# One offset for all blocks of a run, a fourth product in two halves, and other room for a tile's gate weights in a hybrid decoder layer

## The chip, the cores and the metric

The kernel runs on one core of a Trainium2 chip. What counts is the device time of one execution in microseconds (us). The engines that matter are TensorE (PE, with its weight loads as PEld), VectorE (DVE), ScalarE (ACT), GpSimd (POOL) and SyncE (SP), whose queue issues most DMAs.

## The reference

One decoder layer on x of 512 tokens by 1024 channels, in float32: a SwiGLU feed-forward half, a mixer (dilated attention beside a state-space model), and a second SwiGLU half, each between two RMS norms.

```python
h = rms_norm(x, ffn1_pre_g)
x = x + 0.5 * rms_norm(swiglu(h, ffn1_w_in, ffn1_w_out), ffn1_post_g)
h = rms_norm(x, mix_pre_g)
q, k, v, u = split(h @ w_mix_in)
mixed = concat([dilated_attention(q, k, v), s5_mixer(u, ...)]) @ w_mix_out
x = x + rms_norm(mixed, mix_post_g)
h = rms_norm(x, ffn2_pre_g)
x = x + 0.5 * rms_norm(swiglu(h, ffn2_w_in, ffn2_w_out), ffn2_post_g)

def swiglu(x, w_in, w_out):
    gate, up = split(x @ w_in)          # 1024 -> 2 x 2816
    return (silu(gate) * up) @ w_out    # 2816 -> 1024
```

## The kernel before

**Numbers in two parts.** A float32 matrix product is made as three TensorE products: every operand is cut into a high half (a cast to fp32r) and a low half (the rest), and hi·hi, hi·lo and lo·hi are added in one PSUM bank. For weights `wsplit` does it: ScalarE casts `wraw` to `whi` (L117), then DVE or POOL (`pool=True`) subtracts and writes `wlo` (L119). `mm` (L144) issues every product, so nearly all of TensorE's rows have that line, and tiles tell them apart. `mm3` issues the three products.

**Rooms and offsets.** `halves` (L99) gives the next `whi` and `wlo` tiles, out of four rooms each, 1088 elements wide. Of these 1024 are used, from element 0, or from element 16 (`APART`) with `apart=True`. `wraw` has three rooms. A room is free again when the last product that reads it is done. `pad` (L107) takes bytes in a pool so that the tiles behind it lie at other addresses.

**Feed-forward halves.** The 22 tiles of 128 hidden channels are made in two ways. The first 8 (6 in the second half) go one by one, as a gate and an up product with 512 moving columns (`gu`, function `products`). The others go two at a time in `pair` (L598), by a scheme with seven block products in place of eight: `times` (L584) issues one block, 24 products of 128x128 weights with 256 moving columns, into the banks `wx`, `wy` or `wq`. The moving operands are tiles `bh`/`bl` and `tq`, made ahead by `sums`. Between stretches of pairs stand the output products (`yo`, 512 columns); a stretch of pairs between two of them is called a run here. There are five runs, of 3, 4, 3, 3 and 2 pairs; `lead` is true in the first pair of each. In this pair the first block's weights (`a11`) are cut with `apart=not lead`, at element 0; all other blocks at element 16.

**Boundaries.** `boundary` (L273) joins two parts of the layer: it makes the last four k-tiles of the output product (`yt`, 256 columns, the "tail", two halves of the tokens), the norms, the residual, and the first products of the next part (`first`, 256 columns). Between them stand `st` (sums for a norm, 2 columns) and `rp` (spreading the norm's factor, 128 columns). The tail's first products, into the two banks `b2`, are issued by the loop at L330 to L334: k-tiles 0 to 2 for both banks, then k-tile 3. The four chunks of weights for `first` take all four rooms of `whi` and `wlo`.

**Second half.** In `swiglu_half` (L643) tiles 0 and 1 come from the boundary; tile 2 is the third, whose gate weights are loaded by `products(2)`. Pool `fin` holds `gp`, `wx`, `wsum`, `wa` and the `tq` tiles `tq00` to `tq21` of `sums`. The `hooks` put small work between products: `xt` transposes, `st` and `rp` of the boundary's last norm.

**Order.** Instructions wrapped in `fix` keep the order in which they are written; the framework's scheduler orders the others on each engine by its own estimates, and gives each tile its place and its waits.

Of the kernel before, what the change touches and what calls it, by code (L numbers as in the profile page):

```python
# [9 lines left out]
F32R = mybir.dt.float32r  # L10
# [7 lines left out]
P = 128  # L18
S = 512
D = 1024  # L20
KD = D // P
# [11 lines left out]
HT = S // 2  # L33
# [11 lines left out]
class Layer:  # L45
# [227 lines left out]
    def boundary(self, y, tail, ipost, half, inext, chunks):  # L273
# [3 lines left out]
        w = [self.load(c, (KD, P), pool=i % 2 == 1, apart=True) for i, c in enumerate(chunks)]  # L277
        tw = lambda i, m, k: self.tw[m // 2][i].rearrange("p (m k j) -> p m k j", k=NT, j=P)[:, m % 2, k]
        hs = [slice(0, HT), slice(HT, S)]
# [5 lines left out]
        bank, acc = [None], [self.acct(), self.acct()]  # L285
# [43 lines left out]
        b2 = [self.bank("yt")[:, :HT] for _ in range(2)]  # L329
        for ks in (range(NT - 1), (NT - 1,)):  # L330
            for m in range(2):
                for k in ks:
                    th, tl = tail(k)
                    self.mm3(b2[m], tw(0, m, k), tw(1, m, k), th[:, hs[0]], tl[:, hs[0]], k == 0, k == NT - 1)  # L334
        for m in range(2):
            gather(0, m, 1, b2[m].unsqueeze(1))
        squares(0, 0, 2, V)
        for m in range(2, KD):
            b = product(0, m)
            if m % 2 or m > 5:  # L340
                m, n = (m - 1, 2) if m < 6 else (m, 1)
# [3 lines left out]
        for m in range(KD):  # L345
            b = product(1, m)
# [157 lines left out]
    def seven(self, fin, w_in, ig, r, ah, al):  # L504

        nc, V = self.nc, self.nc.vector
        more = [fin]  # L510
        wsum = lambda: more[0].tile([P, 1024], F32, name="wsum", tag="wsum", bufs=3)
        wx = lambda: fin.tile([P, 1024], F32, name="wx", tag="wx", bufs=2)
        gp = lambda: fin.tile([P, 1024], F32, name="gp", tag="gp", bufs=2)
        tq = []
        v4 = lambda t: t.rearrange("p (k c) -> p k c", c=HT)
        blocks = []

        def sums(early=False):

            q = [[gp(), gp()], [wx(), wx()]]  # L520

            def scaled(i):
                for j in range(2):
                    c = slice(j * HT, (j + 1) * HT)
                    for k in range(4):
                        V.scalar_tensor_tensor(out=v4(q[i][j])[:, k], in0=self.x(4 * i + k)[:, c],
                                               scalar=self.g(ig, 4 * i + k), in1=r[:, c], op0=ALU.mult, op1=ALU.mult)
                return q[i]

            b11, b12 = scaled(0)  # L530
            b21, b22 = scaled(1)
            more[0] = (yield) or fin
            self.pad(more[0], 192)
            tq.extend([more[0].tile([P, 1024], F32R, name="tq", tag=f"tq{i}{j}") for j in range(2)] for i in range(3))
            n1, n2, t4 = wsum(), wsum(), wsum()
            V.tensor_tensor(out=n1, in0=b11, in1=b12, op=ALU.subtract)
            yield
            bh, bl = [self.b16(n, F32R) for n in ("bh", "bl")] if early else (None, None)
            v = lambda t, i: t.rearrange("p (q k) c -> p q (k c)", q=4)[:, i]

            def plain(*ts):
                for t in ts:
                    i = len(blocks)
                    blocks.append((v(bh, i), v(bl, i)))
                    self.split(*blocks[i], t)

            if early:
                plain(b11)
            V.scalar_tensor_tensor(out=n2, in0=n1, scalar=-1.0, in1=b22, op0=ALU.mult, op1=ALU.subtract)
            if early:  # L550
                plain(b21)
            yield
            V.scalar_tensor_tensor(out=t4, in0=n2, scalar=-1.0, in1=b21, op0=ALU.mult, op1=ALU.subtract)
            self.split(*tq[0], n2)
            t3 = wsum()
            V.tensor_tensor(out=t3, in0=b22, in1=b12, op=ALU.subtract)
            yield
            if early:
                plain(b22, n1)
            yield  # L560
            self.split(*tq[1], t3)
            yield
            self.split(*tq[2], t4)
            if not early:
                yield
                bh, bl = [self.b16(n, F32R) for n in ("bh", "bl")]
                plain(b11, b21, b22, n1)
            yield

        def block(f, up, kh):  # L570
            if up:
                t = wx() if kh else more[0].tile([P, 1024], F32, name="wa", tag="wa")
            else:
                t = self.wp.tile([P, 1024], F32, name="wraw", tag="wraw", bufs=3)
            src = w_in[f + NF * up:f + NF * up + 2, :, kh * S:(kh + 1) * S].rearrange("f p c -> p f c")
            nc.sync.dma_start(out=t.rearrange("p (f c) -> p f c", f=2), in_=src)
            return t

        def cut(t, pool=False, apart=True):
            hi, lo = self.halves(apart)  # L580
            self.wsplit(t, hi, lo, pool)
            return hi, lo

        def times(bank, w, xb, first):  # L584
            for g in range(2):
                for k in range(4):
                    c, m = slice(k * HT, (k + 1) * HT), slice((4 * g + k) * P, (4 * g + k + 1) * P)
                    st = first and g == 0 and k == 0
                    for i, (wi, xi) in enumerate(((0, 0), (0, 1), (1, 0))):
                        self.mm(bank[:, g * HT:(g + 1) * HT], lhsT=w[wi][:, m], rhs=xb[xi][:, c],  # L590
                                start=st and i == 0, stop=g == 1 and k == 3 and i == 2, skip_group_check=True)

        def keep(bank):
            t = self.tmp("kp")
            nc.scalar.copy(out=t, in_=bank)
            return t

        def pair(f, lead=False, late=False):  # L598
            (b11, b21, b22, n1), (n2, t3, t4) = blocks, tq
            add = lambda x, z, t: V.tensor_tensor(out=t, in0=x, in1=z, op=ALU.add)  # L600
            p2 = lambda t: t.rearrange("p (f c) -> p f c", f=2)
            half = lambda t, h: t[:, :, h * HT:(h + 1) * HT]
            gt = p2(gp())
            X = self.bank("wx")
            a11 = block(f, 0, 0)
            times(X, cut(a11, apart=not lead), b11, True)
            s1 = keep(X)
            a12 = block(f, 0, 1)
            h12 = cut(a12, True)
            Y = self.bank("wy")  # L610
            times(Y, h12, b21, True)
            V.tensor_tensor(out=half(gt, 0), in0=p2(Y), in1=p2(s1), op=ALU.add)
            a21, a22 = block(f, 1, 0), block(f, 1, 1)
            c3 = wsum()
            add(a11, a21, c3)
            c2 = wsum()
            add(c3, a22, c2)
            times(X, cut(c2), n2, False)
            s2 = keep(X)
            c1 = wsum()  # L620
            add(a21, a22, c1)
            Q = self.bank("wq")
            times(Q, cut(c1), n1, True)
            q = keep(Q)
            times(X, cut(c3), t3, False)
            V.tensor_tensor(out=q, in0=X, in1=q, op=ALU.add)
            add(c2, a12, c2)
            times(Q, cut(c2), b22, False)
            V.tensor_tensor(out=half(gt, 1), in0=p2(Q), in1=p2(s2), op=ALU.add)
            nc.scalar.activation(out=gt, in_=gt, func=AF.Silu)  # L630
            times(X, cut(a22, True), t4, False)
            s = f % RING
            dst = lambda t, h: half(t.pair(slice(s, s + 2)), h)
            for h, u in ((1, q), (0, X)):
                V.scalar_tensor_tensor(out=half(gt, h), in0=p2(u), scalar=-1.0, in1=half(gt, h), op0=ALU.mult, op1=ALU.mult)
                if late:
                    self.split(dst(ah, h), dst(al, h), half(gt, h))
            if not late:
                self.split(ah.pair(slice(s, s + 2)), al.pair(slice(s, s + 2)), gt)

        return sums, pair

    def swiglu_half(self, first, scope):  # L643
# [3 lines left out]
        w_in, w_out, w_tail = (self.a["w2" + t] for t in "iot")  # L647
        fin = scope.enter_context(self.tc.tile_pool(name="fin", bufs=1))
        hook = self.tokens_first(fin)
        o0, _, r, late = first  # L650
        ah, al = self.ktiles("ah", F32R), self.ktiles("al", F32R)
        o = {f: o0[2 * f:2 * f + 2] for f in range(len(o0) // 2)}
# [4 lines left out]
        def products(f):  # L657
            o[f] = []
            for i, c in enumerate((f, NF + f)):
                w = self.load(w_in[c], (KD, P), pool=i == 1)  # L660
                b = self.bank("gu")
                self.mmk(b, w, self.xh, self.xl, hooks=hooks.get((f, i), {}))
                o[f].append(b)
# [833 lines left out]
```

## Time and profile before

| | |
|---|---|
| time, median of 3 runs | 931.43 us (930.51 to 931.89) |
| the profiled execution's own time | 930.17 us |
| its span, first to last instruction | 928.3 us |
| PE busy | 912.5 us (98%), 6162 products |
| DVE, ACT, POOL busy | 650.9, 442.4, 214.1 us |
| mean granted TensorE clock | 0.997 |
| HBM read, written | 96.13 MB, 9.70 MB |

Times in the profile are microseconds from the span's start. The page groups instructions by line, engine and tiles. The chain that ended last is followed back from the last instruction, at each step to what released it; in order of time, each piece has a start, a length, and the number of instructions merged in it. In a timeline a row has start, length (several instructions of one kind are merged, with their count), engine, line, operation, `out<-in` tiles and shapes; the idle time before it and what ended it stand in brackets. In the table of windows the columns are the stretch, its length, the busy time of PE, PEld, DVE, ACT and POOL with the number of instructions, the granted clock, the DMA engines' busy share, and GB/s. A TensorE row's length is longer than the gap to the next start, since products are pipelined: the pace is read from starts, or from a chain piece's length over its count.

### The profile page before, as it was taken

To read this page: it belongs to the slowest core of one execution; us is meant where nothing else is said; L and a number is where in the kernel's file an instruction comes from. 1 tells how busy PE (TensorE), PEld (TensorE's weight loads), DVE (VectorE), ACT (ScalarE), POOL (GpSimd) and SP (SyncE) were. 2 spreads that over 40 slices of the span, in tenths; PEclk is the share of its full clock that TensorE was granted. 3 is DMA by queue.
4 is the path that set the end of the run, shared out by engine and by line. 5 is a ranking of instruction groups with operands and counts; after the bars stand their busy time and mean duration, and the time that the engine had idled before them with its cause. 6 is when DMAs were issued, how large, how long until landed. Compare 5 with 4: busy or idle time off the path is not lost.

```text
span 928.3 us, 15349 instructions
## 1 busy us (share of the span) xinstructions
PE 912.5 (98%) x6162; PEld 815.1 (88%) x6162; DVE 650.9 (70%) x1071; ACT 442.4 (48%) x685; POOL 214.1 (23%) x127
## 2 busy tenths in 40 slices
PE   9999999999999999999999999899999999999997
PEld 7887789998999989978777899788899989998995
DVE  6999685755577666758898568698357457745856
ACT  6263764552355543525746554473255414541542
POOL 0423202222222134500000025422222212221321
PEclk9999999999999999999999999999999999999999
DMA  8223662324231252292322441245223322332222
GB/s 271 94 69 114 204 239 88 108 90 133 83 120 41 68 195 80 91 232 94 114 69 73 158 134 47 80 148 181 91 92 115 114 91 91 114 114 91 92 91 90
DMA packets 47734, 106.81 MB, mean 115 GB/s; under 512 B 7824, under 2 KB 11152, under 8 KB 47120
## 3 DMA queue, kind: packets, MB, share of 16 engines
q1 hardware_dynamic: 46080, 102.21, 34.1%
q10 hardware_dynamic: 1584, 3.63, 1.1%
q8 instruction: 48, 0.79, 0.3%
q14 instruction: 22, 0.18, 0.1%
HBM read 96.13 MB, written 9.70 MB: 114 GB/s over the span
## 4 chain that ended last, share of the span: by engine, by line
PE 82%; DVE 4%; DMA 1%; issue 1%; ACT 1%; POOLq 0%; POOL 0%; DVEq 0%; SPq 0%; ACTq 0%
PE yo L144 21%; PE wx L144 18%; PE wq L144 9%; PE yt L144 6%; PE gu L144 5%; PE wy L144 5%; PE first L144 5%; PE prj L144 4%; PE prv L144 2%; PE mo L144 2%; PE st L144 1%; PE ys L144 1%; DMA w1d<-w1s 1%; PE pt L1087 1%; DVE wlo L119 1%
## 5 line engine op out<-in xcount | busy, mean ns | idle before, releaser
L117 ACT CAST whi<-wraw 128x1024 fp32r<-128x1024 f32 (+5 forms) x129 | 125.0, 976 | 167.3 <-PE yo L144 65.5
L119 POOL TENSOR_TENSOR wlo<-wraw,whi 128x1024 fp32r<-128x1024 f32 (+1 forms) x41 | 109.6, 2673 | 305.3 <-ACT whi L117 298.0
L119 DVE TENSOR_TENSOR wlo<-wraw,whi 128x1024 fp32r<-128x1024 f32 (+5 forms) x88 | 107.9, 1233 | 86.3 <-ACT whi L117 86.2
L144 PE MATMUL wx<-tq,whi 128*128 128x256 f32 x720 | 129.3, 281 | 0.0
L144 PEld LDWEIGHTS wx<-tq,whi 128*128 128x128 f32 x720 | 110.5, 190 | 0.0
L119 DVE TENSOR_TENSOR wlo<-wsum,whi 128x1024 fp32r<-128x1024 f32 x60 | 73.2, 1220 | 46.8 <-ACT whi L117 46.8
L117 ACT CAST whi<-wsum 128x1024 fp32r<-128x1024 f32 x60 | 62.9, 1048 | 88.2 <-PE yo L144 28.1
L144 PE MATMUL wx<-tq,wlo 128*128 128x256 f32 x360 | 101.2, 281 | 0.0
L119 POOL TENSOR_TENSOR wlo<-wx,whi 128x1024 fp32r<-128x1024 f32 x15 | 39.2, 2611 | 183.2 <-ACT whi L117 183.2
L144 PE MATMUL gu<-xh,wlo 128*128 128x512 f32 x176 | 69.5, 395 | 4.6 <-DVE wlo L119 3.5
L144 PE MATMUL gu<-xh,whi 128*128 128x512 f32 x176 | 71.3, 405 | 0.0
L144 PE MATMUL gu<-xl,whi 128*128 128x512 f32 x176 | 69.3, 394 | 0.0
L144 PEld LDWEIGHTS wx<-tq,wlo 128*128 128x128 f32 x360 | 67.6, 188 | 0.0
L144 PE MATMUL wq<-bh,whi 128*128 128x256 f32 x240 | 67.4, 281 | 0.0
L144 PE MATMUL wq<-bl,whi 128*128 128x256 f32 x240 | 67.4, 281 | 0.0
L144 PE MATMUL wq<-bh,wlo 128*128 128x256 f32 x240 | 67.4, 281 | 0.0
L144 PE MATMUL yo<-ah,whi 128*128 128x512 f32 x144 | 56.3, 391 | 0.0
L144 PE MATMUL yo<-al,whi 128*128 128x512 f32 x144 | 56.1, 389 | 0.0
L144 PE MATMUL yo<-whi,ah 128*128 128x512 f32 x144 | 56.0, 389 | 0.0
L144 PE MATMUL yo<-wlo,ah 128*128 128x512 f32 x144 | 56.0, 389 | 0.0
L144 PE MATMUL yo<-ah,wlo 128*128 128x512 f32 x144 | 56.0, 389 | 0.0
L144 PE MATMUL yo<-whi,al 128*128 128x512 f32 x144 | 56.0, 389 | 0.0
(261 smaller groups left out, 2380.7 us busy)
## 6 DMA issues: line engine op xcount, KB each, us to landing
wraw<-w1i SPq DMA_DIRECT2D x28, 512.0 KB, 3.7
wraw<-w2i SPq DMA_DIRECT2D x28, 512.0 KB, 3.9
wraw<-w2o SPq DMA_DIRECT2D x18, 512.0 KB, 4.0
wraw<-wmi SPq DMA_DIRECT2D x12, 512.0 KB, 4.0
wraw<-w1o SPq DMA_DIRECT2D x8, 512.0 KB, 4.1
wa<-w2i SPq DMA_DIRECT2D x8, 512.0 KB, 3.6
wx<-w2i SPq DMA_DIRECT2D x8, 512.0 KB, 4.0
wa<-w1i SPq DMA_DIRECT2D x7, 512.0 KB, 3.6
```

Of the source, the lines that this page charges most:

```text
L117: fix(self.nc.scalar.copy(out=hi, in_=raw))
L119: fix(eng.tensor_tensor(out=lo, in0=raw, in1=hi.bitcast(F32), op=ALU.subtract))
L144: i = self.nc.tensor.matmul(*a, **k)
L1087: self.fix(nc.tensor.transpose(b[i][:, o:o + P], sc[:, c:c + P], self.ident))
```

## The change

- `cut` always uses `apart=True`; the first block of a run lies at element 16 like the others.
- In `times`, for the first block of a run (`parted`, given as `lead`), the fourth product (first group, second k-tile, hi·hi) is issued as two products with the same weights, of columns 0 to 127 and 128 to 255.
- In `boundary`, the fourth product of the tail (bank 0, k-tile 1, hi·hi) is issued in the same way in two.
- In `swiglu_half`, the gate weights of tile 2 are cut into two tiles of `fin` with the tags `tq20` and `tq21`, not into rooms of `whi` and `wlo`. These places are used again later by `sums`. The pad of 192 bytes is now taken first in `fin`; `sums` takes it only in the first half (`early`).

```diff
@@ boundary
             for m in range(2):
                 for k in ks:
                     th, tl = tail(k)
+                    if (m, k) == (0, 1):
+                        for a in (0, P):
+                            self.mm(b2[m][:, a:a + P], lhsT=tw(0, m, k), rhs=th[:, a:a + P], start=False, stop=False,
+                                    skip_group_check=True)
+                        self.mm(b2[m], lhsT=tw(0, m, k), rhs=tl[:, hs[0]], start=False, stop=False)
+                        self.mm(b2[m], lhsT=tw(1, m, k), rhs=th[:, hs[0]], start=False, stop=False)
+                        continue
                     self.mm3(b2[m], tw(0, m, k), tw(1, m, k), th[:, hs[0]], tl[:, hs[0]], k == 0, k == NT - 1)
@@ seven
-            self.pad(more[0], 192)
+            if early:
+                self.pad(more[0], 192)
...
-        def cut(t, pool=False, apart=True):
-            hi, lo = self.halves(apart)
+        def cut(t, pool=False):
+            hi, lo = self.halves(True)
...
-        def times(bank, w, xb, first):
+        def times(bank, w, xb, first, parted=False):
             for g in range(2):
                 for k in range(4):
-                    c, m = slice(k * HT, (k + 1) * HT), slice((4 * g + k) * P, (4 * g + k + 1) * P)
+                    m = slice((4 * g + k) * P, (4 * g + k + 1) * P)
                     st = first and g == 0 and k == 0
                     for i, (wi, xi) in enumerate(((0, 0), (0, 1), (1, 0))):
-                        self.mm(bank[:, g * HT:(g + 1) * HT], lhsT=w[wi][:, m], rhs=xb[xi][:, c],
-                                start=st and i == 0, stop=g == 1 and k == 3 and i == 2, skip_group_check=True)
+                        for a, b in ((0, P), (P, HT)) if parted and (g, k, i) == (0, 1, 0) else ((0, HT),):
+                            self.mm(bank[:, g * HT + a:g * HT + b], lhsT=w[wi][:, m], rhs=xb[xi][:, k * HT + a:k * HT + b],
+                                    start=st and i == 0, stop=g == 1 and k == 3 and i == 2, skip_group_check=True)
...
-            times(X, cut(a11, apart=not lead), b11, True)
+            times(X, cut(a11), b11, True, lead)
@@ swiglu_half
         hook = self.tokens_first(fin)
+        self.pad(fin, 192)
...
-                w = self.load(w_in[c], (KD, P), pool=i == 1)
+                into = [fin.tile([P, 1024], F32R, name="tq", tag=f"tq2{j}") for j in range(2)] if (f, i) == (2, 0) else None
+                w = self.load(w_in[c], (KD, P), into, pool=i == 1)
```

## The prediction

> **What bounds the kernel now.** First the page: its engines' shares and the chain that ended last.
>
> ```profile
> span 928.3 us, 15349 instructions
> ...
> PE 912.5 (98%) x6162; PEld 815.1 (88%) x6162; DVE 650.9 (70%) x1071; ACT 442.4 (48%) x685; POOL 214.1 (23%) x127
> ...
> PE 82%; DVE 4%; DMA 1%; issue 1%; ACT 1%; POOLq 0%; POOL 0%; DVEq 0%; SPq 0%; ACTq 0%
> ```
>
> TensorE (PE) is busy 98% and is 82% of the chain, so time is won in two ways only: shorter gaps from one product's start to the next, or fewer waits of PE. The wide pieces of the chain are `yo` (512 columns), then `wx`, `wq` and `wy`, the 256-column products of the pairs. Next, the table of windows for one pair, to see whether anything but PE could be its limit.
>
> ```profile
> 784.58:804.37 19.79, 19.79 (x171) 19.79 (x169) 15.02 (x15) 10.71 (x12) 5.48 (x3) 1.00 0.32 106
> ```
>
> PE is busy 19.79 of 19.79 us; VectorE (DVE) 15.02, ScalarE 10.71, GpSimd 5.48, DMA engines 32%, clock full. So within a pair the pace of PE alone decides. Then the chain in order of time (start, us, what, count), in which equal products can be compared.
>
> ```profile
> 150.39 2.87 PE wx L144 x24
> 167.39 5.65 PE wx L144 x48
> ...
> 343.44 15.55 PE yt L144 x132
> 361.29 5.46 PE yt L144 x48
> 366.75 4.08 PE first L144 x36
> 372.06 2.93 PE first L144 x24
> 375.44 9.54 PE first L144 x84
> ...
> 418.29 7.14 PE st L144 x64
> ...
> 542.20 14.45 PE yt L144 x125
> ```
>
> Dividing us by count: all these but `st` are products of 128x128 weights with 256 columns, yet they come at three paces. The first block of a run: 2.87/24 = 119.6 ns. The rest of a run: 5.65/48 = 117.7 ns; `yt` at 343.44 the same, 15.55/132 = 117.8. And `yt` at 361.29 (5.46/48 = 113.8) and `first` at 366.75 (4.08/36 = 113.3) and 375.44 (9.54/84 = 113.6) run faster, while `first` at 372.06, the same tiles, does not (2.93/24 = 122, its first gap among them). So size alone does not set the pace, nor the tile: the stream has states, and something ahead of it selects one. What stands ahead is in the timeline of PE:
>
> ```profile
> 358.83 0.50 PE L144 MATMUL st<-ones,acc 128*128 128x2 f32 x4
> 359.19 0.36 PE L144 MATMUL yt<-ah,tw 128*128 128x256 f32 x1
> ...
> 360.69 0.61 PE L144 MATMUL rp<-ident,p 128*128 128x128 f32 x4
> 361.05 0.37 PE L144 MATMUL yt<-ah,tw 128*128 128x256 f32 x1
> ```
>
> Behind four 128-column products (`rp`, 360.69) comes the 113.5 ns state; behind four 2-column ones (`st`, 358.83) the slow one. The chain of the next microseconds has the same pair, `st` ahead of the slow `first` and `rp` ahead of the fast one:
>
> ```profile
> 370.83 1.23 PE st L144 x12
> ...
> 374.99 0.44 PE rp L144 x4
> ```
>
> The state also outlasts a change of tiles: `yt` at 361.29 goes over into `first` at 366.75 without leaving it. A run of pairs enters from 512-column products instead:
>
> ```profile
> 150.00 0.39 PE L144 MATMUL yo<-ah,wlo 128*128 128x512 f32 x1
> 150.23 0.28 PE L144 MATMUL wx<-bh,whi 128*128 128x256 f32 x1
> 150.34 0.28 PE L144 MATMUL wx<-bl,whi 128*128 128x256 f32 x1
> 150.46 0.28 PE L144 MATMUL wx<-bh,wlo 128*128 128x256 f32 x1
> ```
>
> Its first gap is 0.11, the next 0.12, and then 119.6 until the block with the other offset of its weights, from which on it is 117.7.
>
> Last, the one large wait, at the start of the second FFN half (timeline around 590):
>
> ```profile
> 588.07 2.94 ACT L117 CAST whi<-wraw 128x1024 fp32r<-128x1024 f32 x3
> ...
> 588.21 2.27 DVE L526 SCALAR_TENSOR_TENSOR gp<-x,sm,rs 128x256 f32<-128x256 f32 x3 [2.42 <-ACT rs L215]
> ...
> 589.74 0.60 PE L498 MATMUL xt<-ident,x 128*128 128x128 f32 x4
> 590.14 2.53 POOL L119 TENSOR_TENSOR wlo<-wraw,whi 128x1024 fp32r<-128x1024 f32 x1 [0.34 <-ACT whi L117]
> 590.40 3.36 DVE L119 TENSOR_TENSOR wlo<-wraw,whi 128x1024 fp32r<-128x1024 f32 x1
> ...
> 593.81 0.54 PE L144 MATMUL gu<-xh,wlo 128*128 128x512 f32 x1 [3.47 <-DVE wlo L119]
> 594.15 0.63 PE L144 MATMUL gu<-xh,whi 128*128 128x512 f32 x1
> ...
> 597.13 0.59 PE L144 MATMUL gu<-xl,whi 128*128 128x512 f32 x1
> 597.56 0.39 PE L144 MATMUL gu<-xh,wlo 128*128 128x512 f32 x1
> 597.79 0.39 PE L144 MATMUL gu<-xh,whi 128*128 128x512 f32 x1
> ```
>
> The third tile's gate weights are cast at 588.07, when the boundary's last products free a room, and their low half is late (DVE, 590.40 + 3.36): PE stands 3.47 us and then runs eight products at 597.56 - 594.15 = 3.41 us, 0.426 each, where 0.23 (597.79 - 597.56) is usual. The granted clock (third column from the right in the table of windows) is 0.72 there:
>
> ```profile
> 593.80:600.00 6.20, 6.19 (x22) 5.06 (x23) 3.23 (x7) 1.05 (x1) 0.00 (x0) 0.72 0.78 265
> ```
>
> **The change part by part.**
>
> *Pace of the runs.* 15 pairs of 7 blocks of 24 are 2,520 products. Now: five first blocks at 2.87 and 2,400 products at 117.7 ns: 14.35 + 282.5 = 296.85 us. I take it that the two 128-column halves do what `rp` does, so that the runs go at 113.5 (the `first` rows): 286.0. The first three products and the two or so behind the halves still go slow, 5 x 5 x 4.5 ns = 0.1. Term: -10.7. The operation is not in this trace: `rp` is of 128 columns too, but its operands are not cast to fp32r. From below I bound the pace by the 128-column `st` row at 418.29, 7.14/64 = 111.6 ns: 281.2 us, a gain of 15.6. From above by the first blocks' 119.6, since the changed offset, which ended that pace, is taken away: 301.4, a loss of 4.5. I take 113.5, nearest to `rp`, the only row with moving 128 columns ahead of 256.
>
> *The halves themselves.* Five runs and two tails: 7 more products, each with its own weight load. At `rp`'s pace (four records from 360.69 to 361.05 and on, some 112 ns each) a split product takes 0.224 instead of 0.118: +0.106, together +0.75 us. Ends: 0, if a half takes half, and 0.33 each, 2.3 us, if a half costs two such records.
>
> *Tail of the first boundary.* 132 products from 117.8 to 113.5: -0.55. In the second boundary the tail behind 542.20 is fast already (14.45/125 = 115.6 with its start, where PE had waited): 0. If the tail gains nothing, the sum is short by 0.55.
>
> *The third tile's room.* The halves go to two `tq` tiles of `fin`, first in that pool. By the code that place was held by the scan's buffers and the last chunk of the boundary's tail weights, done when the tail's last product is (`first` begins at 564.41). The raw weights are there long before:
>
> ```profile
> 541.03 6.38 SPq L123 DMA_DIRECT2D wraw<-w2i  x3
> ...
> wraw<-w2i SPq DMA_DIRECT2D x28, 512.0 KB, 3.9
> ```
>
> Three transfers issued by 547.4 land by some 551.5. So cast and subtraction can be done 20 us early: the 3.47 us wait and the slow clock go, the latter 3.41 - 8 x 0.227 = 1.6: with the gap's edges -5.3. What is late next: the up weights of this tile, whose cast takes the 588.07 place. Its subtraction is GpSimd's, free at 590.14, 2.53 long: done at 592.7, and PE, having started the tile at 589.17, wants it 24 x 0.227 + four hooks of 0.35 later, at some 596. So 3 us are left. SP's queue: the raw room is free earlier, so the next transfer goes earlier, not later. Nothing waits behind.
>
> But the subtraction now lies in the boundary, where DVE is nearly full (windows; DVE is the column behind the length):
>
> ```profile
> 585.70:588.20 2.50, 0.09 (x2) 1.00 0.00 0
> 564.40:585.70 21.30, 19.33 (x44) 1.00 0.13 38
> ```
>
> 19.33 of 21.30 us, then idle from 585.7. One subtraction is 1.22 us (the group of `wlo` from `wsum`: 73.2 us for 60). Put into the idle stretch it costs nothing; put among the preparations of the second half it delays `first` by up to 1.2. Where it falls is the scheduler's choice; I take half, +0.6. If PE waits, that stall replaces part of the one removed.
>
> ```profile
> L119 DVE TENSOR_TENSOR wlo<-wsum,whi 128x1024 fp32r<-128x1024 f32 x60 | 73.2, 1220 | 46.8 <-ACT whi L117 46.8
> ```
>
> *Offset and pads.* All blocks at the same offset and the pad at the head of `fin` change addresses only; no instruction, no wait. Their price is in the pace bounds above.
>
> *Faster pairs, other engines.* A pair shrinks from 19.79 to 19.07 us; DVE's 15.02 then is 79%. A block's cast starts when the block four before it ends, so it is done more than two blocks ahead. Price 0, and if that cover went, it would be DVE's first.
>
> *Sum:* -10.7 + 0.75 - 0.55 - 5.3 + 0.6 = -15.2. The profiled execution took 930.17 us (span 928.3 and 1.87 around it); it becomes 915.0. The median shown, 931.43, is 1.26 above it: 916.2, said as 916.
>
> By the Trainium skill, page "TensorE: Matmul & The Clock Gate", section "Back-to-back issue gap", the spacing is set by the weight load and the product, so by their sizes, and no history enters. By that rule the halves change no pace, and the case is the first rival below; the trace disagrees in that 256 columns come at 113.5, 117.7 and 119.6 ns, so I give the rule little weight.
>
> **The rivals.**
>
> *The kick does not last, or there is none (927).* The runs go at 117.7 whatever is done. For it: a run changes tiles and weight rooms seven times per pair, where the fast state was seen across one change only, and `st`, small products too, selects the slow state. Against: both boundaries. Sum: five first blocks 5 x 0.04 = -0.2, halves +0.75, room -5.3, DVE +0.6: -4.2, so 927.2.
>
> *Partly (918 to 925).* Some runs of the five go fast. They hold 3, 4, 3, 3 and 2 pairs at 0.72 us of gain each; losing 5 to 12 pairs of 15 gives 3.6 to 8.7 back.
>
> *The runs stay in the first block's pace (932).* The old kick, the change of offset, is gone and the new one has no effect: 119.6 throughout, +4.5 for the runs, +0.75, -5.3, +0.6: +0.55, so 932. For it: the first blocks show 119.6 over 23 products without leaving it. Against: `yt` at 343.44 also enters from 512 columns, with one offset, and goes at 117.8.
>
> *Slower (933.5).* The same pace, and the halves at their upper price: 4.5 + 2.3 - 5.3 + 0.6 = +2.1. It becomes slower by more than 0.2% (1.9 us) once a split costs over 0.3 us more than the whole product, at the runs' and tails' fourth product.
>
> **How the numbers follow.** Forecast 0.60, partly 0.09, no kick 0.14, first block's pace 0.08, slower 0.09. 0.2% is 1.9 us, about what a measurement of this kernel can tell from no change. Faster: 0.60 + 0.09 + 0.14 = 0.83; same 0.08; slower 0.09. The forecast's own range goes from 911.5 (the sum with the pace at 111.6: 916.2 - 4.8) to 919 (the sum with splits at the top, DVE at 1.2 and no gain in the tail: 916.2 + 1.55 + 0.6 + 0.55). For 8 in 10 I take in the partial case and no kick: 911.5 to 928.
>
> **What would show it.** In the changed kernel: rows of 48 `wx` in the chain of 5.45 us instead of 5.65, and a first block of some 2.85 with two 128-column records; if 5.65 or 5.74, the pace steps were wrong. `yt` of the first boundary 15.0 plus the half. No wait at 589 to 594, and `gu` there at 0.23; a `wlo` on DVE (or a cast) before 588, and if PE has gaps in `first`, that is its price. Wrong would make me: 128-column halves in fp32r that take far more than 0.11, or a pace lost at the first change of tiles.

## The result and the profile after

The changed kernel takes 916.97 us (median of 4 executions, 916.19 to 918.0) against 930.97 (4 executions, 929.69 to 931.89): ratio 0.985, with a 95% interval of 0.983 to 0.987. The profiled execution has a span of 914.2 us, 14.1 less than before. In two experiments below (without the halves, and the room alone) the profiled execution ran at a granted clock of 0.556 and 0.752, so that only the times of their other executions are used. First its page.

```profile
span 914.2 us, 15367 instructions
...
PE 898.9 (98%) x6169; PEld 801.4 (88%) x6169; DVE 656.0 (72%) x1071; ACT 442.0 (48%) x685; POOL 217.5 (24%) x127
...
PE 79%; DVE 6%; issue 2%; DMA 2%; ACT 1%; POOLq 0%; POOL 0%; DVEq 0%; SPq 0%; ACTq 0%
```

TensorE has seven products more and is busy 13.6 us less: its products became faster. In the chain its share went down by 3 points and VectorE's up by 2: VectorE has come onto the path somewhere. The chain in order of time (start, us, what, count) shows both.

```profile
150.32 2.87 PE wx L144 x25
...
166.79 5.44 PE wx L144 x48
...
207.59 32.66 PE yo L144 x144
...
338.35 15.11 PE yt L144 x133
...
536.42 14.46 PE yt L144 x125
...
578.72 4.35 PE first L144 x36
```

The rows of 48, in all five runs, take 5.44 us, 113.3 ns a product, where they took 5.65. The first block has 25 products now. The whole first run lasts from 150.32 to 207.59, 57.27 us; its 504 products at 113.33 ns would be 57.12, so the halves and the slower products ahead of them cost 0.15 us a run. The first boundary's tail is 15.11 instead of 15.55, with one product more. Three rows of the chain that the sum needs beside them, of the kernel before:

```profile
582.97 4.35 PE first L144 x36
...
675.67 2.87 PE wx L144 x24
...
899.43 13.64 PE yt L144 x60
```

And the same places after (the third and last stretch of pairs begins and ends):

```profile
667.16 2.87 PE wx L144 x25
...
885.38 13.64 PE yt L144 x60
```

Subtracting starts, stage by stage (before, after, difference, us):

| stage | before | after | difference |
|---|---|---|---|
| up to the first run | 150.39 | 150.32 | -0.07 |
| runs 1 and 2, with the output products between | 193.05 | 188.03 | -5.02 |
| first boundary and mixer (343.44 to 542.20) | 198.76 | 198.07 | -0.69 |
| second boundary (542.20 to 582.97) | 40.77 | 42.30 | +1.53 |
| to the third run (582.97 to 675.67) | 92.70 | 88.44 | -4.26 |
| runs 3 to 5 | 223.76 | 218.22 | -5.54 |
| from there to the end | 28.87 | 28.82 | -0.05 |

The runs give 10.56 us; the third tile's room gives only 4.26 - 1.53 = 2.73. Where the rest of that went is seen in the timeline of the second boundary (start, us, engine, line, operation, tiles; idle time before it in brackets), VectorE's rows first:

```profile
561.89 0.47 DVE L317 SCALAR_TENSOR_TENSOR ymix<-ymix,sm,rp 128x256 f32<-128x256 f32 x1
562.28 1.21 DVE L119 TENSOR_TENSOR tq<-wraw,tq 128x1024 fp32r<-128x1024 f32 x1
563.42 1.34 DVE L167 SCALAR_TENSOR_TENSOR xl<-x,sm,xh 128x256 fp32r<-128x256 f32 x2
```

```profile
563.81 0.36 PE L144 MATMUL first<-xh,whi 128*128 128x256 f32 x1
564.42 0.39 PE L144 MATMUL first<-xl,whi 128*128 128x256 f32 x1 [0.24 <-DVE xl L167]
```

The subtraction of the third tile's gate weights (`tq`, 1.21 us) stands in the middle of the preparations; the `xl` behind it is late, and the `first` that needs it starts 0.61 us after the one before it. VectorE has no slack until the boundary is over, so the delay is carried on, in small waits up to 578.

The second loss is in the table of TensorE's waits from 530 to 606 (us in total, times, longest):

```profile
PE xt L505 <- DVE nv L205: 1.2, 1, 1.2
```

The 3.47 us wait of `gu` for its weights is gone, and `xt` waits 1.2 us in its place, for `nv`, a step of the norm that is 0.15 us long itself. The timeline says why it is late:

```profile
583.95 6.83 DVE L533 SCALAR_TENSOR_TENSOR gp<-x,sm,rs 128x256 f32<-128x256 f32 x4 [2.56 <-ACT rs L215]
...
585.37 5.12 POOL L119 TENSOR_TENSOR wlo<-wraw,whi 128x1024 fp32r<-128x1024 f32 x2
...
592.24 1.27 DVE L533 SCALAR_TENSOR_TENSOR wx<-x,sm,rs 128x256 f32<-128x256 f32 x3
...
593.42 0.15 DVE L205 TENSOR_SCALAR nv<-st 128x2 f32<-128x2 f32 x1
...
593.63 0.66 PE L505 MATMUL xt<-ident,x 128*128 128x128 f32 x4 [1.20 <-DVE nv L205]
```

Four scalings `gp`, of the size of the 0.47 us operation at 561.89, take 6.83 us. Beside them GpSimd makes two subtractions of weights without a pause, where before it made one, from 590.14 on. By the code, the room that the third tile's gate weights had goes to weights that come after them. `nv` stands in VectorE's queue behind the scalings. The granted clock (third from the right) stays at 1.00 behind this wait, where it was 0.72 behind the old one:

```profile
593.80:600.00 6.20, 6.20 (x36) 5.29 (x36) 4.36 (x10) 1.71 (x4) 1.47 (x1) 1.00 0.89 322
```

The Trainium skill, page "SBUF — State Buffer", section "SBUF: two separate sides", says that a VectorE operation with two inputs in SBUF and a GpSimd operation that reads SBUF exclude each other for a whole instruction. The trace agrees: three scalings of the same size take 1.27 us with GpSimd at rest (592.24), four would take 1.7; the four here take 5.1 more, and GpSimd's two subtractions beside them last 5.12.

### The profile page after: what moved, and what is told of

Read it like the earlier page. It is cut to its first block, busy times and chain, and to the rows that moved or that the text cites. A ratio compares the mean times of both kernels' runs of the same rounds, so it can differ in the third digit from the quotient of the medians.

```text
span 914.2 us, 15367 instructions
## 1 busy us (share of the span) xinstructions
PE 898.9 (98%) x6169; PEld 801.4 (88%) x6169; DVE 656.0 (72%) x1071; ACT 442.0 (48%) x685; POOL 217.5 (24%) x127
## 4 chain that ended last, share of the span: by engine, by line
PE 79%; DVE 6%; issue 2%; DMA 2%; ACT 1%; POOLq 0%; POOL 0%; DVEq 0%; SPq 0%; ACTq 0%
PE yo L144 21%; PE wx L144 18%; PE wq L144 9%; PE yt L144 6%; PE wy L144 4%; PE gu L144 4%; PE prj L144 4%; PE first L144 3%; PE prv L144 2%; PE mo L144 2%; PE ys L144 1%; PE st L144 1%; DMA w1d<-w1s 1%; PE pt L1098 1%; PE sc L144 1%
## 5 line engine op out<-in xcount | busy, mean ns | idle before, releaser
L144 PE MATMUL wx<-tq,whi 128*128 128x256 f32 x720 | 124.7, 276 | 0.0
L144 PEld LDWEIGHTS wx<-tq,whi 128*128 128x128 f32 x720 | 108.3, 188 | 0.0
L119 POOL TENSOR_TENSOR wlo<-wx,whi 128x1024 fp32r<-128x1024 f32 x15 | 41.5, 2764 | 176.3 <-ACT whi L117 128.5
L144 PE MATMUL gu<-xh,whi 128*128 128x512 f32 x168 | 67.2, 400 | 0.0
L144 PE MATMUL gu<-xh,wlo 128*128 128x512 f32 x168 | 65.7, 391 | 1.1 <-POOL wlo L119 1.1
L144 PE MATMUL gu<-xl,whi 128*128 128x512 f32 x168 | 65.5, 390 | 0.0
```

The source lines that it names most:

```text
L119: fix(eng.tensor_tensor(out=lo, in0=raw, in1=hi.bitcast(F32), op=ALU.subtract))
L144: i = self.nc.tensor.matmul(*a, **k)
```

## The experiments

Three questions: is it the halves, the common offset, or both, that set the pace; what the room alone is worth; and what makes `xt` wait. The theory that the halves alone kick the stream into its fast pace is H; against it stands that the common offset does it. For the wait, C says that VectorE is held up beside GpSimd; the rival is that TensorE merely arrives earlier. All ratios are to the kernel before.

**Without the halves in the runs** (one offset kept):

```diff
-            times(X, cut(a11), b11, True, lead)
+            times(X, cut(a11), b11, True)
```

> The changed kernel with the halves left out of the runs (kept in the tails); all blocks at one offset. Theory H (the two 128-column halves select the fast state): the five runs never reach it, 48 wx take 5.65 to 5.74 us instead of 5.44, and the time is 2,520 products x 4.3 to 6.2 ns, 10.8 to 15.7 us less 0.55 for the halves, above the changed kernel: 927 to 932 us. Within H: 117.7 ns if the offset change was not needed for it, 119.6 to 120 if it was. Rival O (the one offset makes the pace): 5.44 us for 48 wx and 916 to 917 us.

926.78 us, ratio 0.997 (0.995 to 0.999). That is 9.8 more than with the halves by the two medians, which were not taken side by side, and 11.0 by the two ratios. 2,520 products at 117.7 instead of 113.3 would be 11.1 more, less 5 x 0.11 for the halves: 10.5. At the first block's 119.6 it would be 15.3 more. So the common offset alone leaves the runs at 117.7: it does away with the first block's 119.6 and gives nothing else. (A trace of such a run follows below.)

**The halves, but the first block of a run at element 0 as before:**

```diff
-            times(X, cut(a11), b11, True, lead)
+            times(X, cut(a11, apart=not lead), b11, True, lead)
```

> The changed kernel with the first block of a run back at element 0, the others at element 16, halves kept. Theory H: the halves select the fast state, which outlasts a change of offset as it outlasts a change of tiles: 48 wx in 5.44 us, 917 us, same as the changed kernel. Rival O (the one offset is needed): the change of offset at the second block throws the stream into the 117.7 ns state, 5.65 us for 48 wx, and 917 + 10.5 = 927.5 us.

927.28 us, ratio 0.998 (0.996 to 1.000). The chain:

```profile
150.56 2.97 PE wx L144 x25
...
167.66 5.65 PE wx L144 x48
```

Split, but followed by a change of offset, the first block is at the slow pace (2.97 with the halves' 0.11 in it) and the rest at 117.7. H falls: the halves alone do nothing here either. Against the 930.2 of this chip each part alone leaves a gain of some 3 us (3.4 and 2.9), in which the room and the first tail stand too; only together do they give 10 us more. The wait of `xt` for `nv` is there too, 1.2 us, with the slow pace: so it does not come from the faster runs.

**The third tile's room alone**, on the kernel before:

```diff
+                into = [fin.tile([P, 1024], F32R, name="tq", tag=f"tq2{j}") for j in range(2)] if (f, i) == (2, 0) else None
-                w = self.load(w_in[c], (KD, P), pool=i == 1)
+                w = self.load(w_in[c], (KD, P), into, pool=i == 1)
```

> The kernel before with only the third tile's gate weights in the tq tiles (and the pad ahead of them). Theory: the wait of 3.5 us and the slow clock after it go (-5.3), but the subtraction in the boundary costs PE some 1.5 us in first, and the xt transposes wait some 1.3 us for a bank held up on DVE: -2.5, 928.5 us. Rival: the two new waits belong to the faster tail of the changed kernel and are absent here: -5.3, 925.7 us.

927.83 us against 930.2 on the same chip, ratio 0.998 (0.997 to 1.000): -2.4, near the 2.73 of the table of stages. It is not the 5.3 of the wait that it removes. But the interval reaches no change, and the kernel before varies more on this chip: five of its 29 executions took 925.4 to 926.9 us, the others 928.1 to 932.4; why was not followed.

**The up weights of tiles up to the third subtracted on VectorE**, the changed kernel otherwise:

```diff
-                w = self.load(w_in[c], (KD, P), into, pool=i == 1)
+                w = self.load(w_in[c], (KD, P), into, pool=i == 1 and f > 2)
```

> The changed kernel with the up weights of the third tile subtracted on DVE instead of GpSimd. Theory C (two GpSimd subtractions back to back, 585.4 to 590.5, stretch the two DVE instructions beside them from 0.48 to 2.6 us each, and so the norm's small DVE instruction comes late, whose bank the transposes wait for): one of them is gone, the wait at xt of 1.2 us goes or falls under 0.3, 915.7 us. Rival D (DVE's queue is simply too long there): the added 1.2 us subtraction on DVE makes the wait at xt as long or longer, 917 to 918 us.

916.38 us, ratio 0.986 (0.984 to 0.988). TensorE's waits, and VectorE's timeline:

```profile
PE xt L505 <- DVE nv L205: 0.2, 1, 0.2
```

```profile
584.09 2.09 DVE L533 SCALAR_TENSOR_TENSOR gp<-x,sm,rs 128x256 f32<-128x256 f32 x3 [2.58 <-ACT rs L215]
586.10 4.56 DVE L119 TENSOR_TENSOR wlo<-wraw,whi 128x1024 fp32r<-128x1024 f32 x2
```

The wait falls from 1.2 to 0.2, though VectorE has one subtraction more: three scalings take 2.09 us without a GpSimd subtraction at their side, four took 6.83 with it. C holds, and a queue that is simply too long is out. One GpSimd subtraction is left (2.59 us from 586.98), now beside VectorE's two, which take 4.56 us where two of 1.21 are usual. The time shows no gain: it is 0.6 below the changed kernel's, within both intervals, and by the ratios (0.986 and 0.985) it is not lower.

**The changed kernel again**, on the chip of the next three:

> The changed kernel itself, on the same chip as the next runs: 917 us, PE waits of some 1.5 us in first (564 to 578) and 1.3 us at xt (592).

916.57 us, ratio 0.985 (0.984 to 0.986).

**The gate weights' subtraction behind the boundary's preparations:** in the boundary it loses its fixed place, and in the second half it is fixed where its tile is loaded; the up weights on VectorE as above.

```diff
-                pre[0][0](fixp=fx)
+                pre[0][0](fix=lambda i: i if half else fx(i), fixp=fx)
...
-                w = self.load(w_in[c], (KD, P), into, pool=i == 1)
+                w = self.load(w_in[c], (KD, P), into, pool=i == 1 and f > 2, fix=self.fix if into else lambda i: i)
```

> The changed kernel with the third tile's gate subtraction put on DVE behind the last preparation and the norm's small instruction of the boundary (by keeping these in written order), into DVE's idle stretch, and the up weights subtracted on DVE. Theory (the 1.5 us that first waits is the subtraction among the preparations, and the 1.3 us at xt is GpSimd beside DVE): both go, 917 - 2.8 = 914.2 us. Rival (first waits on the preparations themselves, since PE comes sooner to them than before): first keeps its 1.5 us, only xt goes: 915.7 us.

915.65 us, ratio 0.984 (0.982 to 0.985), the shortest of all. The chain:

```profile
151.40 2.87 PE wx L144 x25
...
559.96 4.08 PE first L144 x36
...
565.27 2.93 PE first L144 x24
...
568.65 9.54 PE first L144 x84
...
578.53 4.35 PE first L144 x36
```

The timeline of VectorE:

```profile
582.03 1.23 DVE L119 TENSOR_TENSOR tq<-wraw,tq 128x1024 fp32r<-128x1024 f32 x1 [0.69 <-ACT tq L117]
```

`first` is back in the pieces of 4.08, 2.93, 9.54 and 4.35 us of the kernel before, and the boundary's length with them (537.74 to 578.53, 40.79 us; 40.77 before); the subtraction lies in VectorE's idle time: the 1.53 us of the boundary are this one operation. The wait of `xt` is 0.8 us here, with one `gp` of 2.62 us again beside a GpSimd subtraction. So by the trace 1.5 us came back and 0.4 more. But in this profiled execution the first run starts 1.08 us later (151.40 and 150.32), ahead of all that is changed, and the time is only 0.9 below the changed kernel's on the same chip, with intervals that overlap (0.9822 to 0.9849 and 0.9836 to 0.9862). Whether it is faster is not settled.

**Where the halves stand.** One execution (919.07 us), in which each run has a place of its own. Theory S, formed after the second experiment: at an offset the stream has one or more paces; a shorter product, or a wait, puts it into the faster; a change of the offset puts it back. If so, place and size of the split are open, and only what follows it matters.

```diff
+        if run == 0:
+            offs[0] = 0
+            kick = {1: (four, two)}
+        elif run == 1:
+            offs[1] = 0
+            kick = {0: (four, two)}
+        elif run == 2:
+            kick = {0: ((0, 0, 1), two)}
+        elif run == 3:
+            kick = {0: ((1, 0, 0), two)}
+        else:
+            kick = {0: (four, ((0, 64), (64, HT)))}
```

`offs` are the elements at which the seven blocks of the run's first pair begin (16 elsewhere); `kick` tells the block, the product in it (group, k-tile, term) and its parts.

> One look; the five runs differ. Run 1: first block at element 0 unsplit, halves at the fourth product of the second block (element 16, as all later). Run 2: halves in the first block, second block alone at element 0. Run 3: halves at the second product (hi.lo) of the first block. Run 4: at its 13th. Run 5: the fourth product split in 64 and 192 columns. Theory S (the offset decides which states there are: 113.3 and 117.8 ns at element 16, 120 at 0; the halves choose between the two where there are two): run 1 goes at 113.3 from its second block (2.72 us for 24); run 2 leaves it for 120 in block 2 and comes back to 117.8, not 113.3. Rival F (what matters is that nothing changes after the halves): run 2's later blocks at 113.3 or block 2 at 113.3. If any small product does, runs 3, 4, 5 go at 113.3; if the place or the size counts, at least one of them stays at 117.8. Time between 917 and 928 us.

The chain; lines are shifted, so that L165 is `mm`'s:

```profile
149.35 2.87 PE wx L165 x24
152.22 2.87 PE wy L165 x25
...
165.97 5.44 PE wx L165 x48
...
239.43 2.87 PE wx L165 x25
242.30 2.88 PE wy L165 x24
...
256.48 5.65 PE wx L165 x48
```

Run 1: first block at element 0, unsplit, 119.6; the halves in the second block, at element 16; 113.3 from there on. Run 2: halves in the first block, at 16, which at 2.87 for 25 is as fast as in the changed kernel; then one block at element 0, at 120, and from there 117.7, never 113.3 again. In runs 3 to 5 the second product, the thirteenth, or the fourth in 64 and 192 columns are split, and all go at 113.3. So a change of offset ends the fast pace and the halves behind it set it; place and size make no difference that can be seen. S holds here, with one run of one execution for each case.

**Which offsets.** One execution (927.75): the runs 1 to 5 have all blocks at element 0, 8, 32, 48 and 16, each with halves; in run 5 the fifth product is split.

```diff
+    offs, kick = [(0, 8, 32, 48, 16)[run]] * 7, {}
```

> One look; each run has one offset for all its blocks, and the halves at the fourth product: element 0, 8, 32, 48 in runs 1 to 4; run 5 at element 16 with the fifth product (hi.lo) split in place of the fourth. Theory S: at element 0 the halves do nothing, 120 ns throughout (2.88 us for 24), as in the first blocks of the kernel with two offsets; at 8, 32 and 48 unknown, each either 113.3 (the state exists) or 117.8 to 120. Rival (the offset does not matter as long as it is one): 113.3 in all of runs 1 to 4. Run 5: 113.3 if any early product may be split, 117.8 if the fourth is special.

The chain (L155 is `mm`'s), one row of 48 for each run in order, and the second boundary's tail among them:

```profile
166.78 5.76 PE wx L155 x48
...
259.81 5.68 PE wx L155 x48
...
542.54 14.99 PE yt L155 x125
...
691.06 5.69 PE wx L155 x48
...
783.52 5.65 PE wx L155 x48
...
875.15 5.44 PE wx L155 x48
```

120.0, 118.3, 118.5, 117.7 and 113.3 ns: the pace differs with the offset, and of these five only element 16 reaches 113.3. The tail shows a case against S. Its code is that of the changed kernel, and TensorE waits 0.31 us ahead of it, yet its 125 products take 14.99 us, where they took 14.46 behind a wait of 0.57: a wait does not always lead to the fast pace.

**More offsets, and element 16 without halves.** One execution (929.38): elements 16, 64, 48, 24 and 16; halves only in runs 2 and 4.

```diff
+    offs, kick = [(16, 64, 48, 24, 16)[run]] * 7, {}
+    if lead and run in (1, 3):
+        kick = {0: ((0, 1, 0), ((0, P), (P, HT)))}
```

> One look; each run has one offset for all blocks. Run 1: element 16 without halves. Run 2: 64 with halves at the fourth product. Run 3: 48 without halves. Run 4: 24 with halves. Run 5: 16 without halves. Theory S (the offset decides which states there are, the halves choose): runs 1 and 5 at 117.8 ns throughout (2.83 us for 24), first block too, as far as PE never waits in them; run 3 at 117.8, as it was with halves, so that the halves did nothing there; run 2 at 120 if the offsets repeat after 64 elements (256 bytes), at 113.3 if after 16 or 48; run 4 anything from 113.3 to 120. Rival (a first block at one offset already goes 119.6, as at element 0): runs 1 and 5 at 119.6 to 120.

The chain (L153 is `mm`'s):

```profile
150.10 2.83 PE wx L153 x24
...
259.50 5.76 PE wx L153 x48
...
784.04 5.63 PE wx L153 x48
```

Runs 1 and 5, at 16 without halves: 117.7 from the first block on, so that the reading of the first experiment stands on a trace. Element 64 goes like element 0 (120.0): by this one pair, what counts repeats after 64 elements of 4 bytes. Run 3, element 48 without halves, has 117.7 as with them (rows not shown). Element 24: 117.3. Elements 0, 16 and 48 were seen in two places of the program, with the same paces; 8, 24, 32 and 64 in one run each, where place and offset cannot be told apart. Nor was it tested whether the addresses of the moving operands count: the first tail's `yt`, with weights from element 0 of tiles of their own, goes at 117.8 before and at 113.6 with its half (15.11 less 0.11, for 132).

**Element 16 for all weights that go through the rooms**, on the version with the late subtraction: is 16 better for 512 columns too?

```diff
-    def halves(self, apart=False):
+    def halves(self, apart=True):
```

(likewise in `wtiles` and `load`)

> The kernel with the late subtraction, and all other whi and wlo rooms (the 512-column products gu, yo, prj, mo too) at element 16 instead of 0. Theory: 512-column products have one pace, 226.7 ns for every pair of tiles in these traces, whatever the offset: 144 yo in 32.66 us, 915 to 916 us. Rival (they too have a faster state that the offset 0 shuts out): yo at 220 ns, 144 in 31.7 us, and some 1,700 such products x 6.7 ns = 11 us less, 904 us.

923.43 us, ratio 0.993 (0.991 to 0.995), 7.8 slower than the same version with element 0; both theory and rival had it no slower. The chain:

```profile
209.28 33.59 PE yo L144 x144
...
728.02 32.96 PE yo L144 x144
...
778.04 5.65 PE wx L144 x48
...
859.00 2.72 PE wx L144 x24
...
870.15 5.65 PE wx L144 x48
```

The 512-column products go at 233.3 ns, against 226.8 at element 0 (32.66/144); in the second half, where by the code the rooms hold the moving operand and not the weights, at 228.9. And run 4 stays at 117.7 in spite of its halves, while run 5 starts at 113.3 and falls to 117.7 in its first pair, in a block (2.89 us) where TensorE comes a little late. That alone is not the cause: the changed kernel has such a block in the same place (2.83 at 858.06) and goes on at 113.3. `yo` (3.65 us) and the runs 4 and 5 (3.31) make up some 7 of the 8.3 us by which the span is longer; the rest was not followed. Against S: neither halves nor a wait lead to the fast pace every time. Why runs 4 and 5 differ is open: the runs 1 to 3 too come behind 512-column products at element 16, and go at 113.3 throughout.

## Why the prediction was right

The forecast was 916.2 us, a gain of 15.2; measured were 916.97 and 14.0. By stages, the runs gave 0.4 us more than their terms, the first tail what was said, stages that the sum does not name 0.4 more, and the room 2.0 less.

*Pace.* The step "the halves do what `rp` does, so that the runs go at 113.5" came out: 113.3, and the runs gave 10.56 us where the two first terms said 10.7 - 0.53 = 10.2. The bounds of 111.6 and 119.6 were not reached. But the reason was half of it. "Offset and pads change addresses only; no instruction, no wait" was wrong in what it left out: with the first block at element 0 the halves give nothing (927.28), so that the common offset is as much a condition as the halves. The forecast held because the change does both; as the prediction gave the common offset no part in it, that was luck. "The state also outlasts a change of tiles" is right, and a change of offset is what it does not outlast.

*Halves.* Predicted 0.106 each and 0.02 a run for slow products ahead of them; measured 0.15 a run, both together. The timeline shows the split as one row of two:

```profile
150.51 0.34 PE L144 MATMUL wx<-bh,whi 128*128 128x128 f32 x2
150.68 0.33 PE L144 MATMUL wx<-bl,whi 128*128 128x256 f32 x1
150.86 0.28 PE L144 MATMUL wx<-bh,wlo 128*128 128x256 f32 x1
```

From 150.51 to 150.86 are 0.35 us for the split product and the next, two whole ones being 0.235.

*Tails.* First -0.55 + 0.106 = -0.44; measured 15.11 - 15.55 = -0.44. Second 0; its piece of 125 is 14.46 against 14.45.

*Room.* This term was mis-sized, net. The wait of 3.47 us and the slow clock went, as said. But its cause was only half read: the late `wlo` at 590.40 took 3.36 us beside GpSimd's subtraction at 590.14, where 1.21 is usual, so that the price of GpSimd beside VectorE stood in a row that the prediction shows. The price of the subtraction among the preparations, taken as 0.6 with a top of 1.2, was 1.53: all preparations behind it are late, and the boundary has no slack to take that up. And "nothing waits behind" failed: GpSimd's subtraction was not late itself, the 3 us of slack were there, but it made VectorE's scalings long, and the norm's `nv` is behind them in VectorE's queue: 1.2 us. -4.7 was said for room and subtraction, -2.73 measured. The prediction looked at who is released by the new work and not at who runs beside it.

*Rivals.* "The kick does not last, or there is none" needs runs at 117.7; with 113.3 in all five it is out, as is "partly". The experiments without halves and with two offsets lie at its 927 (926.78 and 927.28), in part by chance: the kernel before took 930.2 on that chip, and the gains of 3.4 and 2.9 stand against the 4.2 of this rival's sum, whose room was too large. In "Partly (918 to 925)" the least loss of 3.6 gives 919.8, not 918. The first block's pace throughout (932), and the slower case built on it, are out: at element 16 no run of pairs showed 119.6. The split's price, from which the slower case decided (0.3 us), was 0.11 to 0.15.

*The rule set against it.* The Trainium skill, page "TensorE: Matmul & The Clock Gate", section "Back-to-back issue gap", sets the spacing by the weight load and the product. That no history enters was read from its silence. In these runs the same two operations are spaced 113.3, 117.3, 117.7, 118.3, 118.5 and 120.0 ns; here the measurement decides.

## What to carry to other kernels

Where TensorE is full, divide the chain's pieces by their counts and compare products of equal shape: where equal products go at different paces, look at what differs ahead of them and at the offset of their weights within their tile, and try both together, since each alone can give almost nothing (926.78 and 927.28 against 916.97). A wait that is removed frees work on other engines earlier; ask what that work runs beside, above all a GpSimd pass beside VectorE's, and not only whether it is in time. One operation put among preparations without slack costs its whole length and a little more (1.53 us for 1.21).

## What the runs showed of the hardware that was not expected

- In the pairs, a stream of 128x128 weights on 256 columns went at a pace that differs with the offset of the weights in their rooms: 120.0 ns at element 0 and 64, 118.3 at 8, 117.3 at 24, 118.5 at 32, 117.7 at 48. At element 16 two were seen, 117.7 without and 113.3 mostly behind a split product. With 512 columns element 0 is the better of two: 226.8 ns, against 233.3 with the weights at 16 and 228.9 with the moving operand there.
- The state holds over hundreds of products and over changes of tile, and it ended at the change of offset that was tried in it (one run, from 16 to 0 and back). In one run it was not reached in spite of the split, in one it was lost in mid-run, and one tail in the experiment on offsets missed it. Why, and what in the chip has this memory, stays open: no run here looked at it other than through starts of products.
- Scalings of 0.47 us took up to 2.62 us each on VectorE beside GpSimd's subtractions of weights, and a subtraction of 1.21 us took 3.36; each GpSimd subtraction of some 2.5 us cost VectorE 2.1 to 2.6.
